# Weight halves split ahead in the feed-forward, and low halves, norms and branches regrouped, in a two-block model on one core

## The chip, the cores and the metric

The kernel runs on one core of one Trainium2 chip. The metric is the device time of one execution in microseconds. A core has TensorE (PE in the profile; its weight loads are PEld), VectorE (DVE), ScalarE (ACT), GpSimd (POOL) and the queue engine SyncE (SP), and 16 DMA engines between DRAM and the on-chip memory SBUF. Matmuls write to PSUM banks, which VectorE and ScalarE read and free.

## The reference

512 tokens of width 1024 pass through two blocks in float32, batch 1, one layer each.

```
# first block: 16 meta tokens ahead of x
h   = rmsnorm(x, g_pre)
u, q, k, v, o, gi, gf, ga, gb = split(h @ w_in)
y_a = gelu(s5_ssm(u, ...));  y_a = y_a * sigmoid(y_a @ w_glu)
y_b = mlstm(q, k, v, gates) normed per head, * sigmoid(o)
merged = sigmoid(ga) * (y_a @ w_a) + sigmoid(gb) * (y_b @ w_b)
x = x + rmsnorm(merged @ w_out, g_post)
h = rmsnorm(x, g_ffn_pre)
x = x + rmsnorm((gelu(causal_dwconv(h @ w_gate)) * (h @ w_up)) @ w_down, g_ffn_post)

# second block
proj = rmsnorm(x, g_mix) @ w_in                    # q, k, v of head groups A, B, C, D
ya, yb, yc, yd = dilated, stick-breaking, sliding-window and block-sparse attention
x = x + (concat of the four, each rms-normed) @ w_out
x = x + memory_cross_attention(rmsnorm(x), rmsnorm(mem))
x = x + squared_relu_mlp(rmsnorm(x))
return rmsnorm(x, g_final)
```

Here rmsnorm(x, g) is x * rsqrt(mean(x * x) + 1e-6) * g.

## The kernel before

Activations lie with features on the 128 partitions and tokens along the free axis, in 8 tiles of 128 features. Each float32 factor of a matmul is kept as two halves: `hi`, the value rounded to the matmul's type, and `lo`, the rest. `mm3` (L130) adds up hi*hi, hi*lo and lo*hi, so a product of 8 tiles is 24 matmuls.

**Weights.** `weights` (L112) brings a chunk of 128 x 1024 (512 KB) to SBUF and splits it: a DMA on SP's queue into a tile `wst` (three buffers), the high half into `whi` and the low half into `wlo` (three buffers each, unless the caller gives a pool `own`). The high half is an ACT copy (L125), the low half a subtraction on the engine in `self.wlow` (L126). That is VectorE, but GpSimd in the weave of the hybrid attention and in the cross attention; there every second high half is a VectorE copy (L123). 34 chunks are split that way: 12 of w_in2, 4 of w_v2 (A and D) and 8 half-size ones of w_out2 in the weave, 10 in the cross attention.

**Order.** The program is traced as one long list of instructions, and a planner sets the order on each engine ahead of the run (the context is opened with `schedule_with_timeline_sim=True`): among instructions whose inputs and buffers are ready in its model, the one that stands earlier in the program comes first. `keep_in_program_order` and `issue_after` pin a few. On the chip each engine takes its instructions in that order and waits at each for its semaphores. SP's DMAs wait in SP's order, and GpSimd's in GpSimd's.

**The stages**, with the times from the profile's timeline: projections, state-space model and mLSTM (to about 340), merge (to 450), feed-forward gate and up products (to about 705) and down products (to about 850), the hybrid attention (to about 1090), cross attention (to 1180), MLP.

- *End of the mixer.* After the weave of mLSTM and gate products, ACT makes the row factors (L853, L854), and per head and half of the tokens a matmul spreads them (L858), VectorE multiplies (L861) and the result `yb` is split. Then `merge` runs: `branch(f, i)` (L915) multiplies chunk f of w_ab with y_a (i = 0) or y_b (i = 1), in the order (0,0) (1,0) (2,0) (0,1) and so on. At this point three PSUM banks `mx` have been added to the two `mm`.
- *Banks.* `product_bank` (L168) gives products a bank in turn: `mx` and `mm` by turns while `self.pmx` is set, else `mm`, or, while `self.third` is 3, the single bank `rs` every third time.
- *Norms.* `rstd_wide` (L249) sums the squares of 1024 features by a matmul with ones into a bank (the single `rs` unless one is given), takes Ln and Exp on ACT and corrects on VectorE. `post_norm` (L1006) calls it for the first block's output and for the feed-forward's, once per half of the tokens; it then updates x, splits it for the next stage, and `rstd_steps` (L269) uses `rs` twice more for the next norm's factors.
- *Feed-forward.* `merge` returns a list `rest` of pieces (thirds of products, loads, ends, 12 copies of bias lines), which `ffn` (L1062) calls one by one; the gate product is multiplied by the norm's factors on VectorE (L1037), convolved (L1045) and passed through gelu on ACT (L1047), the up product is multiplied with it (L1056), and the result is split.
- *Hybrid.* `plan` lists the products (queries, keys, values, output) that fill between the attention units of each head: first a stage without attention (w_v2 of B, chunks 6, 8 and 7 of w_in2), then the weave, from chunk 9 on. Softmax units: scores L1173, maximum L1178, exponent L1185, scaling L1191, transposes L1195, split L106 and L107, product with the values L1219. Stick-breaking units: L1244 to L1277. The bias tiles come by SP's queue (L1168).
- *Cross attention.* Output chunks of w_out2 are added to x (L1652), x is split (L109, L110), its squares are added up on GpSimd (L241), `rstd_steps` makes the factors (L285 to L288 on VectorE, L294 on TensorE).

Of the kernel before, what the change touches and what calls it, by code (L numbers as in the profile page):

```python
# [63 lines left out]
class Net:  # L64
    def __init__(self, ctx, tc, I, out, dump=None):
# [13 lines left out]
        self.wlow, self.turns = nc.vector, 0  # L79
# [32 lines left out]
    def weights(self, src, shape, own=None):  # L112

        nc = self.nc
        kt, cols = shape
        n = kt * cols
        st = self.wst.tile([P, 1024], FT, name="wst")
        nc.sync.dma_start(st[:, 0:n] if len(src.shape) == 2 else st[:, 0:n].rearrange("p (k c) -> p k c", k=src.shape[1]),
                          src)
        hi, lo = ((own or self.whi).tile([P, 1024], FR, name="whi"), (own or self.wlo).tile([P, 1024], FR, name="wlo"))  # L120
        self.turns += 1
        if self.wlow is nc.gpsimd and self.turns % 2:
            nc.vector.tensor_copy(hi[:, 0:n], st[:, 0:n])  # L123
        else:
            nc.scalar.activation(hi[:, 0:n], st[:, 0:n], AF.Copy)  # L125
        self.wlow.tensor_tensor(lo[:, 0:n], st[:, 0:n], hi[:, 0:n].bitcast(FT), OP.subtract)  # L126
        v = lambda t: t[:, 0:n].rearrange("p (k c) -> p k c", k=kt)
        return v(hi), v(lo)

# [119 lines left out]
    def rstd_wide(self, out, accs, t, width=DM, bank=None):  # L249
# [6 lines left out]
        for j, acc in enumerate(accs):  # L256
            mm = nc.tensor.matmul(ps, self.ones, acc, start=j == 0, stop=j == len(accs) - 1)
            if bank is not None and j == 0:
                self.tc.keep_in_program_order(mm)
# [447 lines left out]
    def mixer(self):  # L707
# [3 lines left out]
        with ExitStack() as es:  # L711
# [23 lines left out]
            with ExitStack() as e2:  # L735
# [4 lines left out]
                with tc.tile_pool(name="tmp0", bufs=1, side="right", reuse_waits="tile") as tmp:  # L740
# [33 lines left out]
                    for (t0, n) in FULL:  # L774
                        known = self.rstd_wide(rs[:, t0:t0 + n], [a[:, t0:t0 + n] for a in self.nacc],
                                               tmp.tile([P, 264], FT, name=f"rw{t0}"),
                                               bank=self.ptr.tile([P, 512], FT, name="tr"))
# [33 lines left out]
            with ExitStack() as e2:  # L811
# [40 lines left out]
                row = self.rows[:, T0:L]  # L852
                nc.scalar.activation(row, row, AF.Ln, scale=1.0 / P)  # L853
                nc.scalar.activation(row, row, AF.Exp, scale=-0.5)  # L854
                for h in range(4):
# [13 lines left out]
            jobs = self.merge(self.pool(es, "memp"), mt, yas, ybs, sga, gb, sgs, a2, b2)  # L869
# [36 lines left out]
    def merge(self, mem, mt, yas, ybs, sga, gb, sgs, a2, b2):  # L906
# [3 lines left out]
        mg = []  # L910
# [3 lines left out]
        def branch(f, i):  # L914

            if f not in ws:
                ws[f] = self.weights(I["w_ab"][f], (8, P))
# [3 lines left out]
            for (t0, n) in TAIL:  # L921
# [5 lines left out]
                if i:  # L927
                    nc.gpsimd.tensor_tensor(gs[0], gs[0], gs[1], OP.add)
                    self.split(mg[f][0][:, t0:t0 + n], mg[f][1][:, t0:t0 + n], gs[0], 0.5)

        for f, i in [(0, 0), (1, 0), (2, 0), (0, 1)] + [
                fi for f in range(1, KT) for fi in ((f, 1), (f + 2, 0)) if fi[0] < KT]:
            branch(f, i)
# [8 lines left out]
        for i, (t0, n) in enumerate(TAIL):  # L942
# [10 lines left out]
            steps = self.post_norm(mt, [y[:, t0 - T0:t0 - T0 + n] for y in yo], accs, t0, n, "g_ffn_pre")  # L953
# [52 lines left out]
    def post_norm(self, pool, ys, accs, t0, n, gnext):  # L1006
# [3 lines left out]
        self.rstd_wide(pr, accs, pool.tile([P, 258], FT, name="prt"))  # L1010
# [52 lines left out]
    def ffn(self, e2, rest):  # L1063
        nc = self.nc
        I = self.I
        with ExitStack() as es:
            self.fp = self.pool(es, "fp")
            self.hid = hid = []
            with ExitStack() as e3:
                self.pmx = self.pool(e3, "pmx3", 3, PS)  # L1070
                for piece in rest:
                    piece()
                self.pmx = None
# [235 lines left out]
    def hybrid(self):  # L1309
# [3 lines left out]
        with ExitStack() as es:  # L1313
# [28 lines left out]
            def pair(f, scale, then, ranges=WHOLE, own=None):  # L1342
# [3 lines left out]
                def load():  # L1346
                    st["w"] = self.weights(I["w_in2"][f], (8, P), own)
# [37 lines left out]
            def values(name):  # L1385
# [11 lines left out]
                def load():  # L1397
                    new_v(name)
                    ws.extend(self.weights(I["w_v2"]["ABD".index(name), c], (4, 256)) for c in range(2))
# [135 lines left out]
            self.wlow = nc.gpsimd  # L1535
            self.vx = self.pool(e2, "vx", 1)
            self.weave([(heads(*hs), expand(jobs)) for hs, jobs in plan[1:]])
            self.wlow = V
# [79 lines left out]
    def cross(self, es, out):  # L1618
# [13 lines left out]
        self.wlow = nc.gpsimd  # L1632
# [95 lines left out]
        self.wlow = V  # L1728
# [213 lines left out]
```

## Time and profile before

| | us |
|---|---|
| median of 3 runs | 1547.41 |
| lowest, highest | 1544.9, 1548.17 |
| the profiled execution | 1552.2 |
| its span, first to last instruction | 1550.5 |
| mean granted TensorE clock in it | 0.989 |

The profile is of one execution. Its page begins with the busy time of each engine; the view of windows gives the same for any stretch, with the granted TensorE clock, the share of time in which the DMA engines were busy and what they moved. A row of the list of waits reads: the waiting engine, tile and line, the one that ended the wait, the total in us, how often, the longest. A row of the timeline reads: start, duration, engine, line, operation, out<-in, shapes, how many in a row, and in brackets the idle time before it and what ended it. Matmuls are pipelined, so a row's duration is longer than its step to the next one. In the 40 equal slices of the span the busy tenths are:

```profile
PE   7999899989989999999999999989789999999996
DVE  6988889777587555555476778888886443344334
ACT  5323356664655333334454556575565431134322
POOL 1157821003341000000142354303432000000001
PEclk9999999999999999999999999999999999999999
DMA  6333332226553232324656122114221233333221
```

### The profile page before, as it was taken

To read this page: it belongs to the slowest core of one execution; us is meant where nothing else is said; L and a number is where in the kernel's file an instruction comes from. 1 tells how busy PE (TensorE), PEld (TensorE's weight loads), DVE (VectorE), ACT (ScalarE), POOL (GpSimd) and SP (SyncE) were. 2 spreads that over 40 slices of the span, in tenths; PEclk is the share of its full clock that TensorE was granted. 3 is DMA by queue.
4 is the path that set the end of the run, shared out by engine and by line. 5 is a ranking of instruction groups with operands and counts; after the bars stand their busy time and mean duration, and the time that the engine had idled before them with its cause. 6 is when DMAs were issued, how large, how long until landed. Compare 5 with 4: busy or idle time off the path is not lost.

```text
span 1550.5 us, 25022 instructions
## 1 busy us (share of the span) xinstructions
PE 1474.9 (95%) x9769; PEld 1326.8 (86%) x9769; DVE 1027.4 (66%) x1946; ACT 728.2 (47%) x1420; POOL 329.9 (21%) x304
## 2 busy tenths in 40 slices
PE   7999899989989999999999999989789999999996
PEld 7899899879988899999999877878788888888886
DVE  6988889777587555555476778888886443344334
ACT  5323356664655333334454556575565431134322
POOL 1157821003341000000142354303432000000001
PEclk9999999999999999999999999999999999999999
DMA  6333332226553232324656122114221233333221
GB/s 204 98 110 94 111 105 77 73 96 194 161 157 116 96 93 92 91 94 139 187 170 199 55 68 69 48 41 144 84 67 42 95 96 95 95 96 95 92 85 55
DMA packets 66431, 161.97 MB, mean 104 GB/s; under 512 B 15100, under 2 KB 24556, under 8 KB 66184
## 3 DMA queue, kind: packets, MB, share of 16 engines
q1 hardware_dynamic: 64936, 157.74, 33.0%
q8 instruction: 77, 1.26, 0.3%
q0 software_dynamic: 288, 1.57, 0.3%
q10 hardware_dynamic: 1088, 1.05, 0.2%
q14 instruction: 42, 0.34, 0.1%
HBM read 153.92 MB, written 10.33 MB: 106 GB/s over the span
## 4 chain that ended last, share of the span: by engine, by line
PE 55%; DVE 10%; ACT 3%; issue 1%; POOL 0%; ACTq 0%; DVEq 0%; POOLq 0%
PE mm L135 6%; PE mm L138 6%; PE mm L136 6%; PE mm L165 5%; PE mm L168 5%; PE mm L167 5%; PE mx L165 4%; PE mx L168 4%; PE mx L167 4%; DVE xl L110 2%; PE mx L135 2%; PE mx L138 2%; PE mx L136 2%; DVE ptl L107 1%; PE tr L1219 1%
## 5 line engine op out<-in xcount | busy, mean ns | idle before, releaser
L126 DVE TENSOR_TENSOR wlo<-wst,whi 128x1024 fp32r<-128x1024 f32 (+2 forms) x227 | 284.4, 1254 | 200.0 <-ACT whi L125 121.5
L125 ACT ACTIVATE whi<-wst 128x1024 fp32r<-128x1024 f32 (+3 forms) x244 | 251.9, 1033 | 290.0 <-PE mm L136 107.5
L167 PE MATMUL mm<-xh,whi 128*128 128x256 f32 (+4 forms) x792 | 228.7, 314 | 2.5 <-DVE u L751 2.3
L168 PE MATMUL mm<-xl,whi 128*128 128x256 f32 (+4 forms) x792 | 229.3, 314 | 0.3 <-DVE xl L110 0.3
L167 PE MATMUL mx<-xh,whi 128*128 128x512 f32 (+3 forms) x584 | 176.5, 324 | 7.5 <-ACT xh L109 6.8
L168 PE MATMUL mx<-xl,whi 128*128 128x512 f32 (+3 forms) x584 | 177.6, 326 | 3.3 <-DVE xl L110 3.2
L167 PEld LDWEIGHTS mm<-xh,whi 128*128 128x128 f32 (+1 forms) x792 | 149.8, 189 | 12.9 <-DVE u L751 2.6
L168 PEld LDWEIGHTS mm<-xl,whi 128*128 128x128 f32 (+1 forms) x792 | 149.7, 189 | 10.6 <-issue 0.6
L135 PE MATMUL mm<-hh,whi 128*128 128x256 f32 (+1 forms) x496 | 139.9, 311 | 0.0
L136 PE MATMUL mm<-hl,whi 128*128 128x256 f32 (+1 forms) x496 | 139.7, 311 | 0.0
L165 PE MATMUL mm<-xh,wlo 128*128 128x256 f32 (+4 forms) x792 | 137.6, 313 | 0.0
L167 PEld LDWEIGHTS mx<-xh,whi 128*128 128x128 f32 x584 | 110.5, 189 | 16.7 <-ACT xh L109 7.1
L165 PEld LDWEIGHTS mm<-xh,wlo 128*128 128x128 f32 (+1 forms) x792 | 114.6, 188 | 10.3 <-issue 0.4
L168 PEld LDWEIGHTS mx<-xl,whi 128*128 128x128 f32 x584 | 110.3, 189 | 14.3 <-DVE xl L110 5.0
L165 PE MATMUL mx<-xh,wlo 128*128 128x512 f32 (+3 forms) x584 | 105.9, 322 | 0.0
L126 POOL TENSOR_TENSOR wlo<-wst,whi 128x1024 fp32r<-128x1024 f32 (+1 forms) x34 | 75.2, 2215 | 124.1 <-PE mm L138 39.8
L135 PEld LDWEIGHTS mm<-hh,whi 128*128 128x128 f32 x496 | 93.5, 189 | 6.2
L136 PEld LDWEIGHTS mm<-hl,whi 128*128 128x128 f32 x496 | 93.6, 189 | 5.8
L1004 POOL TENSOR_TENSOR acc<-acc,osq 128x256 f32<-128x256 f32 (+1 forms) x26 | 24.8, 954 | 345.4 <-ACT osq L1001 345.3
L165 PEld LDWEIGHTS mx<-xh,wlo 128*128 128x128 f32 x584 | 87.1, 187 | 9.1
L138 PE MATMUL mm<-hh,wlo 128*128 128x256 f32 (+1 forms) x496 | 83.9, 310 | 1.3 <-DVE wlo L126 1.3
L138 PEld LDWEIGHTS mm<-hh,wlo 128*128 128x128 f32 x496 | 70.8, 189 | 7.4 <-DVE wlo L126 1.7
(555 smaller groups left out, 3317.3 us busy)
## 6 DMA issues: line engine op xcount, KB each, us to landing
wst<-in_w_in_dram SPq DMA_DIRECT2D x52, 512.0 KB, 3.5
wst<-in_w_down_dram SPq DMA_DIRECT2D x32, 512.0 KB, 3.5
wst<-in_w_mup_dram SPq DMA_DIRECT2D x32, 512.0 KB, 3.5
wst<-in_w_mdown_dram SPq DMA_DIRECT2D x32, 512.0 KB, 3.8
wst<-in_w_gate_dram SPq DMA_DIRECT2D x22, 512.0 KB, 3.5
wst<-in_w_up_dram SPq DMA_DIRECT2D x22, 512.0 KB, 3.5
wst<-in_w_out_dram SPq DMA_DIRECT2D x20, 512.0 KB, 3.6
wst<-in_w_down_dram SPq DMA_DIRECT2D x16, 384.0 KB, 3.6
```

Of the source, the lines that this page charges most:

```text
L107: nc.vector.tensor_tensor(lo, src, hi.bitcast(FT), OP.subtract)
L110: nc.vector.scalar_tensor_tensor(lo, src, gain, hi.bitcast(FT), OP.mult, OP.subtract)
L125: nc.scalar.activation(hi[:, 0:n], st[:, 0:n], AF.Copy)
L126: self.wlow.tensor_tensor(lo[:, 0:n], st[:, 0:n], hi[:, 0:n].bitcast(FT), OP.subtract)
L135: nc.tensor.matmul(ps, ah, bh, start=start and i == 0, stop=False)
L136: nc.tensor.matmul(ps, ah, bl, start=False, stop=False)
L138: nc.tensor.matmul(ps, al, bh, start=False, stop=stop and i == n - 1)
L165: nc.tensor.matmul(ps, wl[:, k], xh, start=False, stop=k == KT - 1)
L167: nc.tensor.matmul(ps, wh[:, k], xh, start=k == 0, stop=False)
L168: nc.tensor.matmul(ps, wh[:, k], xl, start=False, stop=False)
L1004: nc.gpsimd.tensor_tensor(acc, acc, sq, OP.add)
L1219: nc.tensor.matmul(yp[0:64, c0:c1], m[:, j, vc:vc + 64], d[:, j - f0, c0:c1], start=ji == x == 0, stop=ji == len(jobs) - 1 and x == 2)
```

## The change

Five edits.

- *Low halves.* `self.wlow` and `self.turns` are gone: every chunk that `weights` splits has its high half made on ACT and its low half on VectorE.
- *Ready chunks.* `split_early` loads a chunk by GpSimd's DMA queue into a tile `pst`, makes the high half in `phi` on ACT and the low half in place on VectorE, and stores both by GpSimd's queue to a DRAM tile. `ffn` calls it 17 times, spread over all but the last 20 of the `rest` pieces (252 by my count of the lists): for chunks 9, 0, 2, 1, 3, 16, 18, 17, 19, 15, 12, 14, 13 of w_in2 and the two chunks each of w_v2 for B and D (indices 1 and 2 of "ABD"). `pst` and `phi` have one buffer each. In the hybrid attention `weights` is handed the DRAM tile as `ready` and only loads the two halves, by two DMAs on SP's queue, straight into `whi` and `wlo`. w_v2 of B and chunk 9 are loaded before the weave; the 14 others are of the weave. w_v2 of A is not among the ready ones.
- *Branches.* The function `branches` now makes `load` and `branch`. Three loads come ahead of the row factors' two ACT instructions, and the first products (0,0), (1,0), (2,0) right after these, still ahead of the spreading matmuls L858, while the banks are the two `mm` and `rs`. The rest of the order is as before.
- *Post-norm's bank.* `post_norm` after the output product passes `self.product_bank`, so that its sums of squares no longer go through `rs`. `self.pmx` is None when the second of its two calls takes the bank. The post-norm after the down product still uses `rs`.
- *Program order.* The pin in `rstd_wide` hangs on a new argument `late`, which only the call that had it before sets.

```diff
-    def weights(self, src, shape, own=None):
+    def weights(self, src, shape, own=None, ready=None):
...
+        v = lambda t: t[:, 0:n].rearrange("p (k c) -> p k c", k=kt)
+        if ready is not None:
+            hi, lo = ((own or p).tile([P, 1024], FR, name=name) for p, name in ((self.whi, "whi"), (self.wlo, "wlo")))
+            nc.sync.dma_start(hi[:, 0:n].bitcast(FT), ready[0])
+            nc.sync.dma_start(lo[:, 0:n].bitcast(FT), ready[1])
+            return v(hi), v(lo)
         st = self.wst.tile([P, 1024], FT, name="wst")
...
-        self.turns += 1
-        if self.wlow is nc.gpsimd and self.turns % 2:
-            nc.vector.tensor_copy(hi[:, 0:n], st[:, 0:n])
-        else:
-            nc.scalar.activation(hi[:, 0:n], st[:, 0:n], AF.Copy)
-        self.wlow.tensor_tensor(lo[:, 0:n], st[:, 0:n], hi[:, 0:n].bitcast(FT), OP.subtract)
-        v = lambda t: t[:, 0:n].rearrange("p (k c) -> p k c", k=kt)
+        nc.scalar.activation(hi[:, 0:n], st[:, 0:n], AF.Copy)
+        nc.vector.tensor_tensor(lo[:, 0:n], st[:, 0:n], hi[:, 0:n].bitcast(FT), OP.subtract)
         return v(hi), v(lo)
+
+    def split_early(self, pool, key, src):
+
+        nc = self.nc
+        d = self.ready[key] = self.dram.tile([2, P, 1024], FT, name=f"ready{len(self.ready)}")
+        st = pool.tile([P, 1024], FT, name="pst")
+        nc.gpsimd.dma_start(st, src)
+        hi, lo = pool.tile([P, 1024], FR, name="phi"), st.bitcast(FR)
+        self.split(hi, lo, st)
+        for i, t in enumerate((hi, lo)):
+            nc.gpsimd.dma_start(d[i], t.bitcast(FT))
...
-    def rstd_wide(self, out, accs, t, width=DM, bank=None):
+    def rstd_wide(self, out, accs, t, width=DM, bank=None, late=False):
...
-            if bank is not None and j == 0:
+            if late and j == 0:
                 self.tc.keep_in_program_order(mm)
...
                 row = self.rows[:, T0:L]
+                mg = []
+                load, branch = self.branches(mg, sga, gb, a2, b2)
+                for f in range(3):
+                    load(f)
                 nc.scalar.activation(row, row, AF.Ln, scale=1.0 / P)
                 nc.scalar.activation(row, row, AF.Exp, scale=-0.5)
+
+                for f in range(3):
+                    branch(f, 0)
                 for h in range(4):
...
-            jobs = self.merge(self.pool(es, "memp"), mt, yas, ybs, sga, gb, sgs, a2, b2)
+            for f, i in [(0, 1)] + [fi for f in range(1, KT) for fi in ((f, 1), (f + 2, 0)) if fi[0] < KT]:
+                branch(f, i)
+            jobs = self.merge(self.pool(es, "memp"), mt, yas, ybs, mg, sgs)
...
-            steps = self.post_norm(mt, [y[:, t0 - T0:t0 - T0 + n] for y in yo], accs, t0, n, "g_ffn_pre")
+            steps = self.post_norm(mt, [y[:, t0 - T0:t0 - T0 + n] for y in yo], accs, t0, n, "g_ffn_pre",
+                                   self.product_bank)
...
-        self.rstd_wide(pr, accs, pool.tile([P, 258], FT, name="prt"))
+        self.rstd_wide(pr, accs, pool.tile([P, 258], FT, name="prt"), bank=bank and bank())
...
-                for piece in rest:
+                pool = self.pool(e3, "pre")
+                self.ready = {}
+                early = [("f", f) for f in (9, 0, 2, 1, 3, 16, 18, 17, 19, 15, 12, 14, 13)]
+                early[1:1] = [("v", 1, c) for c in range(2)]
+                early[11:11] = [("v", 2, c) for c in range(2)]
+                for i, piece in enumerate(rest):
                     piece()
+                    while len(self.ready) < min(len(early), (i + 1) * len(early) // (len(rest) - 20)):
+                        key = early[len(self.ready)]
+                        self.split_early(pool, key, I["w_in2"][key[1]] if key[0] == "f" else I["w_v2"][key[1], key[2]])
...
-                    st["w"] = self.weights(I["w_in2"][f], (8, P), own)
+                    st["w"] = self.weights(I["w_in2"][f], (8, P), own, self.ready.get(("f", f)))
...
-                    ws.extend(self.weights(I["w_v2"]["ABD".index(name), c], (4, 256)) for c in range(2))
+                    ws.extend(self.weights(I["w_v2"]["ABD".index(name), c], (4, 256),
+                                           ready=self.ready.get(("v", "ABD".index(name), c))) for c in range(2))
...
-            self.wlow = nc.gpsimd
             self.vx = self.pool(e2, "vx", 1)
             self.weave([(heads(*hs), expand(jobs)) for hs, jobs in plan[1:]])
-            self.wlow = V
...
-        self.wlow = nc.gpsimd
         self.me = self.pool(self.ctx, "mlpe", side="right")
```

More of the change, by code (lines that the diff above doesn't have):

```diff
@@ L78, in __init__ @@
         self.pmx, self.turn, self.third = None, 0, 0
-        self.wlow, self.turns = nc.vector, 0
         self.pmm = ent("pmm", 2, PS)
@@ L776, in mixer @@
                                                tmp.tile([P, 264], FT, name=f"rw{t0}"),
-                                               bank=self.ptr.tile([P, 512], FT, name="tr"))
+                                               bank=self.ptr.tile([P, 512], FT, name="tr"), late=True)
                     for i, piece in enumerate(pieces):
@@ L904, in glu_jobs, with branches @@
                      for i in range(2)]
-    def merge(self, mem, mt, yas, ybs, sga, gb, sgs, a2, b2):
+    def branches(self, mg, sga, gb, a2, b2):
         nc = self.nc
@@ L909, in merge @@
         I = self.I
-        mg = []
         free = [8, 9, 10, 11, 12, 13, 14, 15, 0, 1, 2, 3, 4, 5, 6, 7]
@@ L916, in branch @@
             if f not in ws:
-                ws[f] = self.weights(I["w_ab"][f], (8, P))
+                load(f)
             wh, wl = ws[f]
@@ L929, in branch, with load, merge @@
                     self.split(mg[f][0][:, t0:t0 + n], mg[f][1][:, t0:t0 + n], gs[0], 0.5)
-        for f, i in [(0, 0), (1, 0), (2, 0), (0, 1)] + [
-                fi for f in range(1, KT) for fi in ((f, 1), (f + 2, 0)) if fi[0] < KT]:
-            branch(f, i)
+        def load(f):
+            ws[f] = self.weights(I["w_ab"][f], (8, P))
+        return load, branch
+    def merge(self, mem, mt, yas, ybs, mg, sgs):
+        nc = self.nc
+        V = nc.vector
+        I = self.I
         self.xp = self.pool(self.ctx, "xp", side="right")
@@ L1004, in out_tile, with post_norm @@
             nc.gpsimd.tensor_tensor(acc, acc, sq, OP.add)
-    def post_norm(self, pool, ys, accs, t0, n, gnext):
+    def post_norm(self, pool, ys, accs, t0, n, gnext, bank=None):
         V = self.nc.vector
         pr = pool.tile([P, 258], FT, name="prs")[:, 0:n]
-        self.rstd_wide(pr, accs, pool.tile([P, 258], FT, name="prt"))
+        self.rstd_wide(pr, accs, pool.tile([P, 258], FT, name="prt"), bank=bank and bank())
         yield
@@ L1727, in cross @@
                 piece()
-        self.wlow = V
     def mlp_up(self, f, pool, tmp, ranges, own=None):
```

## The prediction

> **What bounds the kernel now.** I read the page first, then the view of windows over the stages, then the list of waits in the stages that lose time, and last the timeline at those waits.
>
> ```profile
> span 1550.5 us, 25022 instructions
> PE 1474.9 (95%) x9769; PEld 1326.8 (86%) x9769; DVE 1027.4 (66%) x1946; ACT 728.2 (47%) x1420; POOL 329.9 (21%) x304
> L126 POOL TENSOR_TENSOR wlo<-wst,whi 128x1024 fp32r<-128x1024 f32 (+1 forms) x34 | 75.2, 2215 | 124.1 <-PE mm L138 39.8
> ```
>
> ```profile
> core 0: us, PE busy (x) PEld busy (x) DVE busy (x) ACT busy (x) POOL busy (x), PEclk, DMA share, GB/s
> 325.00:365.00 40.00, 35.05 (x255) 30.20 (x254) 28.49 (x68) 23.87 (x55) 6.75 (x9) 1.00 0.65 199
> 425.00:475.00 50.00, 43.06 (x339) 41.64 (x338) 43.05 (x67) 28.46 (x63) 25.18 (x27) 0.97 0.49 148
> 475.00:850.00 375.00, 373.62 (x2696) 352.09 (x2695) 219.00 (x296) 163.03 (x222) 27.86 (x30) 1.00 0.42 128
> 885.00:1070.00 185.00, 173.94 (x1038) 148.88 (x1037) 150.87 (x367) 114.38 (x297) 63.47 (x54) 0.98 0.21 65
> 1070.00:1110.00 40.00, 32.49 (x227) 28.53 (x225) 34.83 (x92) 25.60 (x78) 15.07 (x8) 0.91 0.29 92
> 1110.00:1180.00 70.00, 60.95 (x467) 57.00 (x466) 58.51 (x154) 44.83 (x130) 26.06 (x25) 0.98 0.19 65
> ```
>
> TensorE is busy 95% of the span, and the change takes no matmul away, so all it can win is TensorE's idle time and half-clock time. In the feed-forward (475 to 850) there is none: 373.6 of 375 us. It lies at the end of the mLSTM (325 to 365: 5.0 us idle), where the merge passes into the feed-forward (425 to 475: 6.9 us) and in the weave and the cross attention (885 to 1180: 11.1 + 7.5 + 9.1 = 27.6 us). The granted clock falls there too: 0.09 of 40 us, 0.02 of 185 and 0.02 of 70 are 3.6 + 3.7 + 1.4 = 8.7 us. So 36 us is the ceiling of the last three windows. What ends the waits there:
>
> ```profile
> PE mm L135 <- DVE x L1652: 3.8, 3, 1.9
> PE rs L294 <- DVE rc L288: 2.7, 2, 1.6
> PE tr L1219 <- DVE ptl L107: 2.6, 4, 1.3
> PE sc L1173 <- DVE nm L1178: 2.4, 3, 1.4
> PE sc L1256 <- DVE ptl L107: 1.7, 1, 1.7
> PE mm L135 <- DVE qkn L1365: 1.6, 1, 1.6
> PE tr L1274 <- DVE ptl L1267: 1.0, 1, 1.0
> ```
>
> Seven groups, 15.8 us, all ended by VectorE. The timeline says why VectorE was late; two places of it:
>
> ```profile
> 919.46 2.35 POOL L126 TENSOR_TENSOR wlo<-wst,whi 128x1024 fp32r<-128x1024 f32 x1
> 919.66 2.57 DVE L107 TENSOR_TENSOR ptl<-e,pth 128x384 fp32r<-128x384 f32 x1 [0.91 <-ACT pth L106]
> 922.28 0.44 PE L1256 MATMUL sc<-ptl,ntri 128*128 128x384 f32 x1 [1.69 <-DVE ptl L107]
> 1102.71 5.09 POOL L126 TENSOR_TENSOR wlo<-wst,whi 128x1024 fp32r<-128x1024 f32 x2
> 1103.94 4.14 DVE L110 SCALAR_TENSOR_TENSOR xl<-x,par,xh 128x256 fp32r<-128x256 f32 x2 [0.25 <-ACT xh L109]
> 1108.00 0.41 DVE L1652 TENSOR_TENSOR x<-x,mm 128x256 f32<-128x256 f32 x1
> ```
>
> The VectorE subtraction L107 begins 0.2 us after GpSimd's L126 and ends 0.4 us after it: 2.57 us, and TensorE waits 1.69 us for it. At 1102.71 two L126 in a row hold two L110 for 4.14 us, and the next L1652, which frees TensorE's bank, comes only at 1108.00. The 34 low halves on GpSimd cost TensorE time through VectorE.
>
> **Part 1, low halves off GpSimd, 14 chunks of the weave ready.** All 34 L126 on GpSimd go (24 in the weave, 10 in the cross attention). 14 of the weave's 24 arrive from DRAM in halves and cost no engine there (the other 3 of the 17 ready ones, chunk 9 and w_v2 of B, were split on VectorE before the weave; 3 x 1.23 us less there, not counted). 20 go to VectorE, their high halves to ACT: 10 of the cross attention, 2 of w_v2 of A, 8 half-size ones.
>
> ```profile
> L126 DVE TENSOR_TENSOR wlo<-wst,whi x227: 198/1225/2523, 6.0 to 1518.9; 128x1024 fp32r<-128x1024 f32 x105, 128x768 fp32r<-128x768 f32 x8, 128x64 fp32r<-128x64 f32 x1
> L123 DVE CAST whi<-wst x17: 419/682/2897, 872.4 to 1146.1; 128x1024 fp32r<-128x1024 f32 x13, 128x512 fp32r<-128x512 f32 x4
> L107 DVE TENSOR_TENSOR hl<-up,hh 128x512 fp32r<-128x512 f32 x22 | 15.0, 683 | 0.5 <-ACT hh L106 0.4
> L125 ACT ACTIVATE whi<-wst x244: 240/1059/1077, 5.0 to 1517.0; 128x1024 fp32r<-128x1024 f32 x111, 128x768 fp32r<-128x768 f32 x8, 128x512 fp32r<-128x512 f32 x2, 128x64 fp32r<-128x64 f32 x1
> ```
>
> VectorE gains 12 x 1.23 us and 8 x 0.68 us (the 128x512 row) = 20.2 us and loses 13 casts of 0.68 and 4 of 0.42 = 10.5 us: 10 us more of its own work, in 295 us of which it is busy 244. Against it stand the holds: of the seven wait groups I find an L126 at the root of all of L1256 and L1274, of both L288, of two of the three L1652 (3.4), of half of L1219 (1.3), the longest L1178 (1.4) and half of L1365 (0.8): 12.3 us. In the cross attention (L1652, L288, L1219: 7.4 us) the same halves now take 1.23 us of VectorE instead of holding it some 2.4, so I count half, 3.7. That leaves 8.6 us. The half-clock stretches follow such gaps; of 8.7 us I take 3.4. **Part 1: -12 us**; the ends are 0, if other waits close up in their place, and -25, if the holds that I could not trace count too. ACT makes 20 high halves where it made 17: nothing, beside 185 us busy of 295.
>
> [...]
>
> **Part 2, the norm's own bank.** The second post-norm (L1010) shares the single bank "rs" with the factors of the first.
>
> ```profile
> 447.39 0.37 ACT L1001 ACTIVATE osq<-mm 128x256 f32<-128x256 f32 x1
> 454.89 0.42 ACT L106 ACTIVATE kh<-kn 128x256 fp32r<-128x256 f32 x1 [3.04 <-DMA mkd<-kh]
> 455.21 0.37 ACT L296 ACTIVATE rs<-rs 128x258 f32<-128x258 f32 x1
> 457.82 0.47 ACT L260 ACTIVATE prs<-rs,eps 128x256 f32<-128x256 f32 x1
> PE mx L168 <- DVE xl L110: 2.6, 1, 2.6
> ```
>
> Its sums are ready at 447.8 (the last square), but the logarithm L260 starts at 457.8: the bank is held until ACT, 3 us behind a store, has read it in L296. From a bank of its own the chain can start up to 9 us earlier, and the wait for xl (2.6 us) at its end, the crumbs after it (0.9) and the half-clock stretch (0.03 of 50 = 1.5 us) go: 5.0. The bank is one of the two "mm" that the products around it use, so some product waits for an evacuation: +1. **Part 2: -4** (from -5 to +1).
>
> **Part 3, branches ahead of the row norms.**
>
> ```profile
> PE mx L135 <- ACT whi L125: 2.4, 1, 2.4
> PE st L858 <- ACT rows L854: 1.7, 1, 1.7
> 358.59 0.51 ACT L109 ACTIVATE ya<-mem,par 128x256 fp32r<-128x256 f32 x1 [1.79 <-DMA mem<-in_mem_dram]
> 359.31 1.04 ACT L125 ACTIVATE whi<-wst 128x1024 fp32r<-128x1024 f32 x1
> ```
>
> TensorE waits 1.7 us for ACT's two row functions and 2.4 us for a high half that stood in ACT's queue behind inputs of the memory. Loads and first products of three branches, issued earlier, give it work there: **-3** of 4.1 (from -4.1 to +2, since they now use three banks where five were). Late next is the first xl of yb (0.8 us in the same list's window, not counted).
>
> **Part 4, the 17 splits in the feed-forward.** Each is a GpSimd load of 512 KB, a high half on ACT, a low half on VectorE, two GpSimd stores: 17 x 1.06 = 18 us of ACT, 17 x 1.23 = 21 us of VectorE, 51 transfers, 26.7 MB.
>
> ```profile
> L1004 POOL TENSOR_TENSOR acc<-acc,osq 128x256 f32<-128x256 f32 x14 | 12.5, 896 | 329.3 <-ACT osq L1001 329.3
> wst<-in_w_gate_dram SPq DMA_DIRECT2D x22, 512.0 KB, 3.5
> xk<-mkd POOLq DMA_DIRECT2D x1, 1024.0 KB, 5.5
> bias<-ed SPq DMA_DIRECT2D x16, 256.0 KB, 2.6
> ```
>
> What hides them: VectorE and ACT are idle 156 and 212 us in that window, GpSimd has nothing in it for 329 us, the DMA engines are 42% busy. One split is a chain through a single pair of buffers: 3.5 to 5.5 us of load, 1.06, 1.23, and as much again for the stores, 9 to 13 us; 17 take 160 to 225 us, the pieces they are spread over about 230. VectorE may free a bank 1.2 us late, which five banks cover. **+1** (from 0 to +35, rival 3). The ready chunk's two loads in the weave replace one on SP; 24 chunks in 185 us are one in 7.7 us, and three buffers leave two chunks, 15 us, for 7 us of landing: nothing (rival 2).
>
> **Sum.** -12 - 4 - 3 + 1 = -18 us. The profiled execution took 1552.2 us (1.7 around its span); 1552.2 - 18 = 1534.2. It lies 4.8 us above the median of the three runs, 1547.41, so on their scale I forecast **1529.4, say 1529 us** (-1.2%).
>
> **The rivals.** (1) *Other waits close up.* The order on each engine is planned anew, and TensorE waits next for the softmax itself. For it: 15.8 of 27.6 us of idle time are the seven groups, the rest is already something else. Half of part 1 and 2 is then lost: 1537. (2) *SP becomes the gate.* A ready chunk's loads wait for TensorE to release the third chunk back, and the bias loads (2.6 us to landing) stand behind them in SP's queue. Against it: the 15 us above. If each of 14 chunks costs 0.8 us, 11 us of part 1 go: 1541. (3) *Slower.* A high half stands at the head of ACT's queue until its load lands; behind it is the gelu, behind that VectorE's product and the evacuations that free TensorE's banks. It decides once a load lands over some 12 us later than planned (2696 matmuls in 373.6 us are 0.14 us each, 3.3 us for a product of 24; five banks of them are 16.6 us, less some 4 us of VectorE's own work); the landings above speak against it. At 2 us a split it costs 34 us: 1529 + 34 = 1563. (4) *The hold turns round*: ten low halves of 1.23 us each hold GpSimd's squares L241, which the factors wait for: +12, so 1541. (5) *The splits do not stay in the feed-forward* but are planned into 450 to 475, where VectorE ends the wait: three of them, 3.7 us: 1533.
>
> **How the numbers follow.** Forecast 0.62, rival 1 0.15, 2 0.06, 3 0.09, 4 0.05, 5 0.03. The range goes from 1512 (all untraced holds and the full clock too) to 1549, which takes in rivals 1, 2, 4, 5 and parts 2 and 3 at their bad ends, and leaves out rival 3 and some of the forecast's best. About 0.2% (3 us) is what a measurement of this kernel tells from no change: faster, under 1544.3: 0.83; same: 0.07; slower: 0.10.
>
> **What would show it.** After: no L126 on GpSimd; VectorE's L107, L110 and L1191 between 885 and 1180 near 0.4 us; TensorE's idle time there down from 27.6 to some 17 us; the second L260 within 3 us of the last square; no wait for whi near 360; TensorE still over 99% busy from 475 to 700, with 17 more high halves on ACT. I am wrong if TensorE waits in the feed-forward, if SP's queue ends waits in the weave, or if the idle time of 885 to 1180 stays with new names.

## The result, and the profile after

The changed kernel took **1524.7 us** (median of 4 runs, 1523.58 to 1526.47) beside 1547.79 for the kernel before on the same chip: a ratio of 0.9839, 95% interval 0.981 to 0.9868. On a second occasion it took 1525.17 beside 1549.19, ratio 0.984 (0.9817 to 0.9862). The forecast was 1529 us, 18 us off; 23 to 25 us came off. The profiled execution took 1525.71 us where that of before took 1552.2: 26.5 us. One run of low_gpsimd (2383 us) and one of cross_ready (5034 us) were in a slow state and count in no ratio, clock or rest below.

The head of the page of the kernel after, its busy time by engine, and its costliest group of VectorE:

```profile
span 1524.0 us, 25154 instructions
PE 1464.5 (96%) x9769; PEld 1319.5 (87%) x9769; DVE 1007.3 (66%) x1963; ACT 741.2 (49%) x1437; POOL 284.0 (19%) x321
L127 DVE TENSOR_TENSOR wlo<-wst,whi 128x1024 fp32r<-128x1024 f32 (+3 forms) x244 | 299.2, 1228 | 193.1 <-ACT whi L126 116.9
```

The same 9769 matmuls; all 244 low halves of staged chunks are VectorE's now (227 before). The view of windows of the kernel after, by the same stages as before, which now come earlier (2 us at the last square of the merge, 8 us at the first scores of the weave, 19 us at the last, 26 us in the MLP); the first row of the weave thus begins some 20 us earlier in the work than before, but in those 20 us (865 to 885) TensorE of before was never idle. A row has the stretch and its length, busy us (and instructions) of PE, PEld, DVE, ACT and POOL, granted clock, DMA share and GB/s:

```profile
325.00:365.00 40.00, 38.33 (x284) 33.55 (x284) 30.94 (x72) 25.86 (x57) 7.53 (x8) 1.00 0.55 169
425.00:475.00 50.00, 42.79 (x345) 41.18 (x345) 41.40 (x69) 29.80 (x65) 26.09 (x27) 1.00 0.52 165
475.00:820.00 345.00, 343.67 (x2448) 322.24 (x2447) 219.96 (x287) 163.38 (x216) 48.28 (x72) 1.00 0.59 197
865.00:1050.00 185.00, 183.22 (x1144) 160.50 (x1143) 136.08 (x378) 119.67 (x309) 16.45 (x32) 1.00 0.35 113
1050.00:1090.00 40.00, 35.45 (x264) 30.83 (x262) 34.54 (x105) 29.90 (x85) 4.62 (x5) 1.00 0.34 113
1090.00:1165.00 75.00, 70.02 (x526) 64.02 (x527) 62.34 (x164) 50.59 (x142) 19.98 (x25) 1.00 0.21 72
```

- TensorE's idle time in the weave and the cross attention is 1.8 + 4.6 + 5.0 = 11.3 us where it was 27.6: **-16.3**. At the end of the mLSTM it is 1.7 where it was 5.0: **-3.3**.
- From the merge into the feed-forward (425 to 475) it is 7.2 where it was 6.9: nothing won there.
- The granted clock is full in every one of these rows. Before, the rows of 425, 885, 1070 and 1110 lost 1.5 + 3.7 + 3.6 + 1.4 = 10.2 us: **-10.2**. That is this one execution; a second profiled one of the same kernel (after_again) had a clock of 0.99 from 865 to 1050 us and of 0.96 from 1050 to 1090, some 3.4 us, so the means over the runs, further down, are the better measure.

That is 29 us, against 26.5 in the whole; some 3 us came back in other places, among them a gap where the weave's first loads stand (3.9 us idle between 820 and 865, with the one half-clock stretch that is left between 325 and 1500; in the second profiled execution it was 2.1 us without a stretch). There TensorE waits 0.8 us for a ready chunk's load (`wlo<-ready`), 1.1 us in the second execution: ready chunks have a small cost of their own, ahead of the weave.

What TensorE still waits for between 865 and 1165, the longest of the list of waits (total us, times, longest):

```profile
PE mm L146 <- ACT oh L105: 1.6, 2, 0.8
PE sc L1206 <- DVE nm L1211: 1.5, 5, 0.5
PE mm L146 <- DVE x L1683: 1.1, 2, 0.7
PE mm L146 <- DVE x L1712: 1.1, 2, 0.9
```

No wait is longer than 0.9 us, and half of them are ended by ACT. And what became of VectorE's instructions, groups of the kernel before in the weave and the cross attention, then the same operations after (us busy, mean ns of one):

```profile
L107 DVE TENSOR_TENSOR ptl<-e,pth 128x128 fp32r<-128x128 f32 (+3 forms) x16 | 14.5, 907 | 3.9 <-ACT pth L106 3.8
L110 DVE SCALAR_TENSOR_TENSOR xl<-x,par,xh 128x256 fp32r<-128x256 f32 x26 | 21.7, 839 | 2.1 <-ACT xh L109 2.1
```

```profile
L106 DVE TENSOR_TENSOR ptl<-e,pth 128x128 fp32r<-128x128 f32 (+3 forms) x16 | 8.1, 506 | 3.9 <-ACT pth L105 3.8
L109 DVE SCALAR_TENSOR_TENSOR xl<-x,par,xh 128x256 fp32r<-128x256 f32 x32 | 19.1, 598 | 1.3 <-ACT xh L108 1.2
```

The same subtraction takes 0.51 us where it took 0.91, and the cross attention's xl 0.60 where it took 0.84. (The scaling of the softmax, L1191 before, takes 0.39 where it took 0.52.)

### The profile page after: what moved, and what is told of

Same layout as the page of the kernel before. It is cut to its first block, busy times and chain, and to the rows that moved or that the text cites. A ratio compares the mean times of both kernels' runs of the same rounds, so it can differ in the third digit from the quotient of the medians.

```text
span 1524.0 us, 25154 instructions
## 1 busy us (share of the span) xinstructions
PE 1464.5 (96%) x9769; PEld 1319.5 (87%) x9769; DVE 1007.3 (66%) x1963; ACT 741.2 (49%) x1437; POOL 284.0 (19%) x321
## 4 chain that ended last, share of the span: by engine, by line
PE 65%; DVE 7%; ACT 3%; DMA 2%; issue 1%; DVEq 0%; SPq 0%; ACTq 0%
PE mm L146 6%; PE mm L147 6%; PE mm L149 6%; PE mm L176 5%; PE mm L179 5%; PE mm L178 5%; PE mx L176 4%; PE mx L179 4%; PE mx L178 4%; PE mx L146 3%; PE mx L147 3%; PE mx L149 3%; PE mm L1396 2%; PE mm L1395 2%; PE mm L1393 2%; DVE xl L109 1%
## 5 line engine op out<-in xcount | busy, mean ns | idle before, releaser
L127 DVE TENSOR_TENSOR wlo<-wst,whi 128x1024 fp32r<-128x1024 f32 (+3 forms) x244 | 299.2, 1228 | 193.1 <-ACT whi L126 116.9
L146 PE MATMUL mm<-hh,whi 128*128 128x256 f32 (+1 forms) x480 | 132.6, 307 | 0.0
L147 PE MATMUL mm<-hl,whi 128*128 128x256 f32 (+1 forms) x480 | 132.5, 307 | 0.0
L146 PEld LDWEIGHTS mm<-hh,whi 128*128 128x128 f32 x480 | 90.4, 189 | 5.4
L147 PEld LDWEIGHTS mm<-hl,whi 128*128 128x128 f32 x480 | 90.5, 189 | 5.1
L252 POOL TENSOR_TENSOR nacc<-nacc,sq 128x256 f32<-128x256 f32 (+2 forms) x58 | 56.2, 970 | 202.2 <-ACT sq L251 193.0
L149 PE MATMUL mm<-hh,wlo 128*128 128x256 f32 (+1 forms) x480 | 79.5, 307 | 1.3 <-DVE wlo L127 1.3
L149 PEld LDWEIGHTS mm<-hh,wlo 128*128 128x128 f32 x480 | 67.5, 188 | 6.7 <-DVE wlo L127 1.7
L252 POOL TENSOR_TENSOR acc<-acc,sq 128x264 f32<-128x264 f32 (+1 forms) x6 | 4.3, 741 | 335.3 <-ACT sq L251 335.3
```

Source lines behind the costliest of these rows:

```text
L127: nc.vector.tensor_tensor(lo[:, 0:n], st[:, 0:n], hi[:, 0:n].bitcast(FT), OP.subtract)
L146: nc.tensor.matmul(ps, ah, bh, start=start and i == 0, stop=False)
L147: nc.tensor.matmul(ps, ah, bl, start=False, stop=False)
L149: nc.tensor.matmul(ps, al, bh, start=False, stop=stop and i == n - 1)
L252: (nc.vector if k % len(accs) else nc.gpsimd).tensor_tensor(acc[:, c:c + w], acc[:, c:c + w], sq, OP.add)
```

## The experiments

Every time is a median; "before" is the kernel before on the same chip. "Clock" is the time that the half-speed stretches took from a run: its span times (1 - mean granted clock), averaged over the runs of the kernel; the clock is given to 0.001, so a difference of 1 us says nothing. "Rest" is the mean time less that.

| kernel | us | before | ratio (95%) | clock | rest |
|---|---|---|---|---|---|
| before (11 runs, first call) | 1549.21 | | | 15.8 | 1534.1 |
| low_vector | 1537.89 | 1549.21 | 0.9925 (0.9907 to 0.9942) | 15.9 | 1522.4 |
| no_ready | 1535.51 | 1549.21 | 0.9905 (0.9889 to 0.9921) | 15.6 | 1520.0 |
| splits_unused | 1536.70 | 1549.21 | 0.9914 (0.9901 to 0.9928) | 14.6 | 1522.1 |
| low_gpsimd | 1538.92 | 1549.21 | 0.9927 (0.9913 to 0.9942) | 13.5 | 1525.1 |
| idle_work_both | 1540.75 | 1551.74 | 0.9935 (0.9916 to 0.9954) | 13.3 | 1527.7 |
| idle_work_vector | 1534.55 | 1551.74 | 0.9893 (0.9873 to 0.9913) | 11.5 | 1523.1 |
| no_bank | 1530.44 | 1551.74 | 0.9864 (0.9843 to 0.9885) | 13.0 | 1517.1 |
| branches_late | 1528.81 | 1551.74 | 0.9852 (0.9832 to 0.9873) | 9.5 | 1518.9 |
| after_again (the change) | 1525.17 | 1549.19 | 0.9840 (0.9817 to 0.9862) | 8.4 | 1517.1 |
| cross_ready | 1535.38 | 1549.19 | 0.9902 (0.9880 to 0.9924) | 14.4 | 1520.7 |
| more_ready | 1534.57 | 1549.19 | 0.9898 (0.9875 to 0.9920) | 13.5 | 1521.1 |
| bank_alone | 1547.31 | 1552.10 | 0.9976 (0.9961 to 0.9992) | 13.3 | 1534.7 |

The kernel before had 17.9 and 17.8 us of clock on the occasions where its median was 1551.74 and 1552.10, with a rest of 1533.7 and 1533.8: what varied between these occasions is the clock, by 2.1 us, where the rest stayed within 0.4. So kernels of different calls are compared by their ratios; 0.001 is 1.55 us.

### Low halves, and ready chunks: two halves of part 1

The first, low_vector, is the kernel before with

```
-        self.turns += 1
-        if self.wlow is nc.gpsimd and self.turns % 2:
-            nc.vector.tensor_copy(hi[:, 0:n], st[:, 0:n])
-        else:
-            nc.scalar.activation(hi[:, 0:n], st[:, 0:n], AF.Copy)
-        self.wlow.tensor_tensor(lo[:, 0:n], st[:, 0:n], hi[:, 0:n].bitcast(FT), OP.subtract)
+        nc.scalar.activation(hi[:, 0:n], st[:, 0:n], AF.Copy)
+        nc.vector.tensor_tensor(lo[:, 0:n], st[:, 0:n], hi[:, 0:n].bitcast(FT), OP.subtract)
```

> The kernel before with one edit: all 34 low halves of the weave and the cross attention on VectorE, their high halves on ACT; nothing is made ready early. Theory H (the low halves on GpSimd hold VectorE, and that was most of the gain): at least 15 of the 23 us, 1527 to 1533 us, and TensorE's idle time between 885 and 1180 us well under the 27.6 us of before. Rival W (most of the gain is the splitting work that the ready chunks take out of the weave): VectorE has 34 more low halves there, so 1540 us or more.

The next, no_ready, is the changed kernel without the splits in the feed-forward:

```
                 for i, piece in enumerate(rest):
                     piece()
-                    while len(self.ready) < min(len(early), (i + 1) * len(early) // (len(rest) - 20)):
...
```

> The changed kernel without the 17 early splits: every chunk of the weave is split where it is used, on ACT and VectorE. Theory H: within 6 us of the changed kernel, 1525 to 1531 us. Rival W: 1536 us or more. The feed-forward itself should take the same time as in the changed kernel within 1 us.

Then splits_unused makes and stores them, and the weave doesn't look for them:

```
-                    st["w"] = self.weights(I["w_in2"][f], (8, P), own, self.ready.get(("f", f)))
+                    st["w"] = self.weights(I["w_in2"][f], (8, P), own)
-                    ws.extend(self.weights(I["w_v2"]["ABD".index(name), c], (4, 256),
-                                           ready=self.ready.get(("v", "ABD".index(name), c))) for c in range(2))
+                    ws.extend(self.weights(I["w_v2"]["ABD".index(name), c], (4, 256)) for c in range(2))
```

> The 17 splits are made in the feed-forward and stored, but the weave loads and splits every chunk as if they were not there. Against the run without the splits this prices the splits alone. My prediction's part 4 (hidden but for a little): +0 to +2 us. Rival (they delay banks or transfers of the feed-forward): +4 us or more, and TensorE below 99% busy between 475 and 800 us.

And low_gpsimd is the changed kernel with `self.wlow` and the six old lines of low_vector's diff back, so that the 20 chunks that aren't ready are split with GpSimd again.

> The changed kernel with its 20 low halves that are not ready (10 in the weave, 10 in the cross attention) back on GpSimd, and the casts of every second high half back on VectorE; the 14 ready chunks stay. Theory H: the holds come back for 20 of 34, so 20/34 of some 20 us: 1534 to 1539 us. Rival W: 1525 to 1529 us.

**Neither theory holds alone.** Moving the low halves gives 0.0075, 11.6 us (low_vector), where theory H wanted at least 15 and rival W at most 9; no_ready's 1535.5 us falls between the two as well. (The same lines also take the 17 casts L123 off VectorE; on balance VectorE has more work.) The use of the 17 ready chunks gives as much again: from 0.9914 with the splits unused to 0.984, 11.5 us. The two kinds of gain are different. Windows over the weave and the cross attention, of low_vector, then of no_ready, then of the kernel after:

```profile
870.00:1175.00 305.00, 287.76 (x1884) 255.07 (x1883) 246.10 (x655) 213.89 (x548) 42.53 (x62) 0.98 0.24 72
```

```profile
870.00:1175.00 305.00, 287.94 (x1871) 254.25 (x1870) 244.52 (x653) 212.50 (x546) 41.75 (x62) 0.97 0.23 72
```

```profile
865.00:1165.00 300.00, 288.69 (x1932) 255.35 (x1931) 232.96 (x644) 200.16 (x535) 41.05 (x62) 1.00 0.31 103
```

With the low halves on VectorE TensorE is idle for 17.2 us instead of 27.6, but the clock stays where it was (0.97 to 0.98; 15.9 us a run against 15.8). With the ready chunks it is idle for 11.3 us, and the clock comes back: 8.4 to 9.5 us a run. The holds themselves are gone as soon as the low halves leave GpSimd, although VectorE now makes 36 of them in that stretch: low_vector's L107, which took 0.91 us before,

```profile
L107 DVE TENSOR_TENSOR ptl<-e,pth 128x128 fp32r<-128x128 f32 (+3 forms) x16 | 7.8, 488 | 3.8 <-ACT pth L106 3.5
```

That is 0.91 to 0.49 us with only the engines of the halves edited. By what means a low half on GpSimd holds VectorE these runs don't show.

What TensorE waits for in no_ready, and no longer in the kernel after (list of waits, 870 to 1170):

```profile
PE tr L1248 <- DVE ptl L106: 3.2, 3, 1.2
PE tr L1248 <- ACT pth L105: 2.0, 3, 1.3
PE tr L1303 <- DVE pth L1295: 1.4, 1, 1.4
PE mm L146 <- DVE qkn L1394: 0.7, 1, 0.7
```

None of these four is over 0.4 us in the kernel after, and nowhere in that list does TensorE wait for a chunk's `whi` or `wlo`. Only the last two, 2.1 us, lie where no_ready splits the 14 chunks (some 870 to 985 us). There the low half, and other steps behind it, stand on VectorE ahead of the cast that TensorE waits for:

```profile
950.06 1.23 DVE L127 TENSOR_TENSOR wlo<-wst,whi 128x1024 fp32r<-128x1024 f32 x1
952.76 0.57 DVE L1295 CAST pth<-e 128x512 fp32r<-128x512 f32 x1
953.38 0.69 PE L1303 MATMUL tr<-pth,v2h 128*64 128x512 f32 x1 [1.42 <-DVE pth L1295]
```

A half-clock stretch of 6.83 us begins there too, at 953.08. The kernel after has neither: its TensorE is busy for 125.00 of 125 us from 865 to 990, at full clock. In these two executions that is some 5.5 us. The first two waits stand at 1012 to 1084 us, behind the last of the 14 splits; from there on (990 to 1090 in no_ready, 990 to 1080 in the kernel after) TensorE is idle for 9.1 us against 5.3. The order on each engine is planned anew, and why it comes out better there was not traced.

And low_gpsimd, with 20 of the 34 halves back on GpSimd, loses 0.0087, 13.5 us, as theory H expected: its xl in the cross attention is held again, 0.80 us on average instead of 0.60. So the halves on GpSimd matter, and so does what the weave no longer splits; 11.6 and 11.5 are nearly all of the 25. The splits alone, unused, cost 0.0009, 1.4 us, inside the intervals, and TensorE is busy without a gap beside them (splits_unused, the feed-forward up to 700 us):

```profile
475.00:700.00 225.00, 225.00 (x1465) 205.19 (x1464) 150.82 (x207) 100.74 (x121) 26.11 (x50) 1.00 0.61 210
```

### Is it the engines' time that the ready chunks save?

After each ready chunk's loads, idle_work_both does as much work as a split, into a buffer that nobody reads:

```
             nc.sync.dma_start(lo[:, 0:n].bitcast(FT), ready[1])
+            x = self.wst.tile([P, 1024], FT, name="wst")
+            nc.scalar.activation(x[:, 0:n], hi[:, 0:n].bitcast(FT), AF.Copy)
+            nc.vector.tensor_tensor(x[:, 0:n], x[:, 0:n], lo[:, 0:n].bitcast(FT), OP.subtract)
             return v(hi), v(lo)
```

> The changed kernel, whose ready chunks still come from DRAM, but each of the 17 is followed by a copy on ACT and a subtraction on VectorE of the size of a split, into a buffer that nobody reads. The runs so far put 11 us on the use of the ready chunks (1536.7 with the splits unused, 1524.7 with them used, the kernel before being 1549.2 and 1547.8 on the two occasions). Theory W (what the ready chunks save is the time of ACT and VectorE): the 11 us go, 1533 to 1538 us. Rival C (what they save is the chain of load, high half and low half in front of TensorE): TensorE waits for none of this work, 1524 to 1528 us.

In idle_work_vector the line of ACT is left out, and the subtraction reads `hi`:

> The same with the subtraction on VectorE alone, no copy on ACT. If VectorE is what the ready chunks free: within 3 us of the run with both. If it is ACT: 1524 to 1528 us. Rival C: 1524 to 1528 us as well.

The subtractions alone cost 0.0053, 8 us; with the copies on ACT it is 0.0095, 15 us, more than the 11.5 that the ready chunks give. The intervals of the two runs don't overlap. Neither lies where it was expected: the run with both is above theory W's 1538, and the run with VectorE alone is neither within 3 us of it nor under 1528, so VectorE and ACT both count. Rival C's 1524 to 1528 is missed by both, and in no_ready's waits above TensorE never stands at the chain of load, high half and low half. Where the added work lies (865 to 1000 us) TensorE is idle for 5.2 and 2.5 us; in the kernel after it is not idle there.

So instructions that TensorE never waits for do cost it time. But 8 and 15 us are not the price of their busy time alone: each also stood at the head of its engine's queue until a load had landed. The longest of these waits of TensorE in idle_work_both, with what stood in front of it (timelines of ACT and VectorE):

```profile
PE rs L308 <- DVE rc L302: 2.5, 1, 2.5
872.17 1.06 ACT L122 ACTIVATE wst<-whi 128x1024 f32<-128x1024 f32 x1 [0.90 <-DMA whi<-ready]
873.27 1.23 DVE L123 TENSOR_TENSOR wst<-wst,wlo 128x1024 f32<-128x1024 f32 x1 [2.23 <-ACT wst L122]
```

VectorE worked for 1.23 us there and stood for 2.23. From 865 to 1060 us it stood for 14.8 us in front of the 15 idle subtractions of idle_work_vector, always for a load, and for 12.5 us in idle_work_both (6.0 for loads, 6.5 for ACT's copies). The splits of no_ready waited for no load in that stretch. The idle work also holds the ready and the staging buffers longer. How much of 8 and 15 us is work and how much standing wasn't measured, so these runs show that time on the two engines matters in the weave, and not what a microsecond of it costs.

### The norm's own bank

In the changed kernel, no_bank takes the argument away again; bank_alone adds it to the kernel before:

```
             steps = self.post_norm(mt, [y[:, t0 - T0:t0 - T0 + n] for y in yo], accs, t0, n, "g_ffn_pre",
-                                   self.product_bank)
...
+        self.rstd_wide(pr, accs, pool.tile([P, 258], FT, name="prt"), bank=bank and bank())
```

> The changed kernel with the post-norms' sums back in the one shared bank. My prediction's part 2 (4 us from this bank): 1527 to 1530 us. Rival (a new wait, for VectorE's values that come from the same two banks, took the gain): within 1.5 us of the changed kernel, 1523 to 1526 us.

> The kernel before with one edit: the post-norms' sums in a bank of their own. My prediction's part 2, as it was put: 4 us off, 1543 to 1547 us beside a before of some 1549, with TensorE's idle time between 425 and 475 us down by 3 us or more. Rival (seen in the changed kernel: the wait for xl shrinks and waits for VectorE's values and keys take its place, so the idle time of that stage stays within 1 us, and only a half-clock stretch may go): 1546.5 to 1549.5 us.

The bank alone gives 0.0024, 3.7 us (1.2 to 6.0), and taking it out of the changed kernel costs as much, 0.0024 (with intervals that overlap). But no idle time goes: bank_alone's rest is 1534.7 us against 1533.8, and its clock 13.3 against 17.8; with no_bank the rest is the same as the change's, and the clock is 13.0 against 8.4. Windows and waits from 425 to 475 us of bank_alone, beside the 43.06 us and 0.97 of before:

```profile
425.00:475.00 50.00, 42.92 (x347) 41.30 (x346) 42.35 (x74) 29.34 (x66) 26.14 (x26) 1.00 0.51 158
```

```profile
PE mm L167 <- DVE vl L110: 1.5, 1, 1.5
PE mm L135 <- DVE kn L1585: 1.2, 1, 1.2
PE mx L168 <- DVE xl L110: 0.7, 2, 0.4
```

The wait of 2.6 us for xl shrank to 0.7. A wait of 1.5 for vl, the evacuation of a product's bank, took its place; the idle time is the same 7 us, cut into smaller pieces, and the half-clock stretch that stood here is gone, as the rival had it. In seven profiled executions, by their clock from 430 to 475 us: one begins at 471.6 and 471.5 us in the two without the bank (before, low_vector) and none there in the five with it (bank_alone, after, no_ready, splits_unused, low_gpsimd); another, between 441 and 445, stands in low_vector and in three of the five (no_ready, splits_unused, low_gpsimd).

### The branches ahead of the row norms

In branches_late the loads and first products of the branches are back behind the end of the mLSTM:

```
-                for f in range(3):
-                    load(f)
...
-                for f in range(3):
-                    branch(f, 0)
...
+            for f, i in [(0, 0), (1, 0), (2, 0), (0, 1)] + [
```

> The changed kernel with the branches' loads and first products back behind the end of the mLSTM. My prediction's part 3: 2 to 4 us slower than the changed kernel, 1526.5 to 1529 us, with the wait for a high half near 360 us back. Rival (nothing depends on it): 1523 to 1526 us.

It took 3.6 us more by the medians, 0.0012 (1.9 us) by the ratios, whose intervals overlap; the trace decides. Waits of branches_late from 325 to 370 us, both of which the kernel after has lost (0.3 us of the first is left):

```profile
PE st L869 <- ACT rows L865: 1.7, 1, 1.7
PE mx L146 <- ACT whi L126: 1.6, 1, 1.6
```

### Ten and twelve more chunks

If ready chunks pay by VectorE's time, the cross attention's should be made ready too. In cross_ready ten keys are added, in more_ready twelve:

```
+                early += [("r", 0), ("r", 1), ("r", 2), ("r", 3), ("q", 0), ("q", 1), ("o", 0), ("o", 1), ("m", 0), ("m", 1)]
```

and `ready=self.ready.get(...)` where those weights are used.

> The changed kernel with ten more chunks split in the feed-forward: those that the cross attention still splits itself (four of w_out2, two of w_xq, two of w_xo, two of w_mup). Theory W (ready chunks pay by the VectorE and ACT time that they free where TensorE waits for these two): the 17 gave 11 us, so 10 chunks take 4 to 7 us off, 1518 to 1521 us, out of the 21 us that TensorE loses between 1050 and 1165 us. Rival (27 splits at 11 us each reach past the stretch of the feed-forward that hides them, or the cross attention's waits are the softmax's own chain): 1524 us or more.

> The same with the two chunks of w_v2 for the heads A too, 29 in all. Theory W: 0 to 1.5 us below the run with 27, since TensorE waits hardly at all where these two are split (under 1 us between 875 and 1000 us). Rival (29 chains of 11 us are 319 us and end after the last pieces): slower than the run with 27 by 2 us or more.

**Both are slower than the change, by 0.0062 and 0.0058, 9 to 10 us** (the 0.6 us between them are inside the intervals), and theory W's number for cross_ready is wrong on both sides of the sum. First the cost: the splits, 11 us each, ended at 653 us with 17 and run on to 774 with 27. Windows of cross_ready, then of the changed kernel run beside it:

```profile
650.00:820.00 170.00, 163.50 (x1235) 156.04 (x1234) 108.42 (x130) 86.06 (x125) 39.87 (x53) 0.99 0.71 240
```

```profile
650.00:820.00 170.00, 168.63 (x1297) 162.04 (x1296) 98.34 (x122) 80.75 (x118) 23.16 (x24) 1.00 0.52 154
```

Up to 650 the two are alike, without idle time. After it cross_ready's TensorE is idle for 6.5 us instead of 1.4. The timeline of its ACT at the longest of those waits, and its longest in the list of waits from 650 to 820:

```profile
780.46 0.84 ACT L127 ACTIVATE whi<-wst 128x768 fp32r<-128x768 f32 x1 [4.47 <-DMA wst<-in_w_down_dram]
781.21 0.46 ACT L1022 ACTIVATE yd<-mm,par 128x256 f32<-128x256 f32 x1
781.57 0.37 ACT L1027 ACTIVATE osq<-mm 128x256 f32<-128x256 f32 x1
```

```profile
PE rs L269 <- POOL acc L1030: 3.1, 1, 3.1
```

A high half of w_down stands at the head of ACT's queue for 4.5 us until its load has landed; behind it the evacuation, the square and GpSimd's sum, and TensorE last. Between 700 and 800 us the loads of w_down land after 4.3 us where they took 3.6. Then the gain: from 1050 on the cross attention's TensorE is idle for 9.6 us of 120, beside 9.0 of 115 in the changed kernel, although VectorE and ACT have ten splits less. What is left there are much the same waits as the kernel after has (oh, nm and x), and the time freed on VectorE and ACT did not shorten them.

## Why the prediction was right, and where it was not

- **What bounds the kernel: right.** The time went where TensorE was idle or at half clock, and nowhere else; the feed-forward stayed full. The 23 to 25 us that came off, where 18 were forecast, are the terms below: two of them right, one right in size by luck, and the largest half its size.
- **Part 1, -12 us: too small by about half, and this is the step that was mis-sized.** The low halves alone gave 11.6 us, near the whole term; not as 8.6 idle and 3.4 of the clock, but as 10.4 idle and nothing of the clock. The ready chunks, which the term valued only as work that isn't added ("10 us more of its own work" on VectorE, charged with nothing), gave another 11.5 us. The mistake is the sentence that set VectorE's work against its 244 busy of 295 us and charged nothing for it: time of VectorE and ACT among the softmax's short steps does cost TensorE time. The runs show it from both sides, 11.5 us for taking the splits out and 8 to 15 us for putting idle work (and its loads) in; some 5.5 of the 11.5 are traced, the rest is not. The two together, 23 us, come near the end of -25, but not by holds that couldn't be traced, as the prediction had it.
- **Part 2, -4 us: the size right (3.7 alone), the way wrong, so the size is luck.** The norm's chain does start early: the second norm's logarithm begins 2.2 us after the last square, where it began 10 us after. The 2.6 us of xl went, and a wait for vl took nearly all of it; the term had 1 us for such a thing. What the bank gives is the half-clock stretch, for which the term had 1.5 of its 5.0 us.

```profile
445.40 0.37 ACT L1026 ACTIVATE osq<-mx 128x256 f32<-128x256 f32 x1
447.61 0.45 ACT L271 ACTIVATE prs<-mm,eps 128x256 f32<-128x256 f32 x1
```

- **Part 3, -3 us: right.** 3.3 us of idle time went between 325 and 365; without the edit both waits are back (1.9 us by the ratios, inside the intervals).
- **Part 4, +1 us: right** (1.4, within noise), but with less room than it said: ten more splits cost some 10 us.
- **The clock was counted too low throughout**: 3.4 + 1.5 us of it, where 10 us went in the rows shown, 8 in the whole profiled executions (1550.5 us at 0.989 and 1524.0 at 0.994) and 6 to 7 in the means of all runs.
- **The sum.** The parts one at a time are 11.6 + 11.5 + 3.7 + 1.9 - 1.4 = 27 us; together they gave 25. The difference is inside the intervals.
- **Rivals.** (1) *Other waits close up*: no, the idle time fell by 16.3 us where 10 were forecast. (2) *SP's queue*: no wait of TensorE in the weave was ended by it; ahead of the weave one of 0.8 us was. (3) *The high half at the head of ACT's queue*: not with 17 splits; with 27 it is exactly what happened. The prediction put its point at loads 12 us late; it came with loads 0.7 us late in the median and 4.5 us at the worst wait, in a stretch that already used half of the DMA engines. (4) *The hold turned round*: GpSimd's squares took 0.97 us on average where they took 0.94, 1.5 us in all over 58 (busy 56.2 us in the kernel after, 54.7 before). (5) *Splits before 475*: the first began at 468, and no wait was ended by one.

## What to carry to other kernels

In this weave and cross attention VectorE, busy for 244 of 295 us before and for 233 of 300 after among short dependent steps, had no free time: 21 us of added VectorE work cost 8 us, with the loads that it stood and waited for, and taking some 32 us of splitting out of the weave gave 11.5. Don't enter such work at nothing, and look at what it waits for at the head of the queue as well as at how long it takes. It ends somewhere: ten splits less in the cross attention gave nothing (9.6 us idle of 120, beside 9.0 of 115). And the cover ends somewhere: 17 splits in the feed-forward cost 1.4 us, ten more some 10 us, with the loads of w_down landing after 4.3 us instead of 3.6; measure where it ends before adding more. And read the granted clock beside the idle time: the same 7 us of idle time, cut differently, stood with a half-clock stretch in one kernel (0.97 from 425 to 475 us, before) and with none in another (1.00, bank_alone).

## What the runs showed of the hardware

The half-clock stretches were a larger share than expected, and they follow a fixed beat. Windows of the kernel before, cut at the changes of the clock:

```profile
963.13:966.54 3.41, 3.41 (x19) 3.41 (x17) 2.22 (x5) 2.02 (x5) 1.43 (x3) 0.50 0.08 26
1031.40:1034.81 3.41, 3.41 (x16) 2.92 (x15) 1.82 (x7) 0.97 (x6) 0.00 (x0) 0.50 0.13 47
1079.19:1086.02 6.83, 6.46 (x32) 5.75 (x31) 4.86 (x26) 5.12 (x19) 0.00 (x0) 0.50 0.42 148
1126.97:1130.38 3.41, 3.41 (x19) 3.41 (x18) 2.12 (x5) 1.42 (x4) 0.73 (x1) 0.50 0.00 0
```

Each lasts 3.41 us or twice that, and the distances between their starts are whole multiples of 3.413 us (963.13 to 1031.40 is 20, to 1126.97 it is 48). The stretches aren't tied to places of the program: of two profiled executions of the changed kernel the first has one at 839.00 (0.96 from 820 to 865 us) and a clock of 1.00 from 865 to 1090; the second (after_again) has 1.00 from 820 to 865, 0.99 from 865 to 1050 and 0.96 from 1050 to 1090. So which gaps fall badly changes from run to run. Of the eight stretches of the kernel before one follows 3.41 us in which TensorE is idle throughout, and six follow 3.41 us with only 1.5 to 2.3 us of idle time. The 3.41 us ahead of 963.13 and of 1079.19, and a third piece of the beat with as little work, after which the clock stayed full:

```profile
959.72:963.13 3.41, 1.79 (x14) 1.52 (x13) 3.31 (x6) 3.31 (x7) 1.56 (x2) 1.00 0.43 132
1075.78:1079.19 3.41, 1.95 (x14) 1.46 (x14) 3.34 (x12) 1.80 (x10) 0.92 (x1) 1.00 0.39 108
338.49:341.90 3.41, 1.74 (x14) 1.51 (x13) 1.09 (x3) 3.21 (x4) 0.00 (x0) 1.00 1.01 347
```

And the stretch at 1031.40 follows 3.41 us in which TensorE was busy for 3.25:

```profile
1027.99:1031.40 3.41, 3.25 (x26) 2.64 (x24) 3.35 (x12) 3.36 (x8) 0.00 (x0) 1.00 0.13 34
```

Of its 26 matmuls some 16 are the factors' sums L279, one column wide (two rows of 8 in the timeline); so busy time, as the profile models it, doesn't decide alone. What else does wasn't tested.
